# Hybrid two-layer trunk on one core: gate rows by way of DRAM, mLSTM tables with the maximum folded into the forget gate, one decay sum of 129 columns

## The chip, the cores and the metric

The kernel runs on one core of one Trainium2 chip. The metric is the device time of one execution in microseconds (us). The kernel before takes 2866.2 us, the median of three runs (2865.12 to 2867.47 us). Engines are named as the profile names them: PE is TensorE (PEld its weight loads), DVE VectorE, ACT ScalarE, POOL GpSimd, SP SyncE, which issues the DMAs.

## The reference

A trunk of two layers over x, 256 tokens of 2048 channels in float32. Each layer is a token mixer and a SwiGLU feed-forward network (FFN), and each of these four sub-layers ends in the same way:

```python
x = LayerNorm(ALPHA * x + (1 + gate(c)) * f(x * (1 + scale(c)) + shift(c)))
```

Shift, scale and gate are products of SiLU(c) with large modulation weights, 48 tiles of 1 MB for each sub-layer. In layer 0 the mixer is half mLSTM (8 heads of 128 channels) and half RWKV-7 (16 heads of 64), in layer 1 half retention and half gated DeltaNet.

What the change touches is, first, the gate: 2048 numbers, one for each channel, by which every token's row is multiplied. Second, the mLSTM gates. With lf the log-sigmoid of the forget gate and ig the input gate, in the form that both kernels compute:

```python
m[t] = max(lf[t] + m[t-1], ig[t])                      # running maximum, m[-1] = 0
table[s, t] = exp(lf[s+1] + ... + lf[t] + ig[s] - m[t])   # for s <= t
h = (q k^T * table) v / max(|row sum|, exp(-m[t]))
```

Third, RWKV-7's decay: for each channel the running sum of the log decay over time, and the exponentials of it and of its negative.

## The kernel before, in words

Everything stays in one core's on-chip memory but the weights, which stream in once. All large products follow one pattern. A weight tile of 1 MB (`raw`, three buffers) is loaded by SP (L327), split in two halves into a rounded part `hi` on ACT (L340) and the rest `lo` on DVE (L341), and PE multiplies each half by the activations with three matmuls per step (L360 `hi` x high part, L361 `lo` x high part, L362 `hi` x low part), 24 matmuls for a tile, called a unit below. Products gather in the four `g` banks of PSUM. Behind each unit `fill` lets in modulation tiles at a set rate: each is a 1 MB load into a `raw` buffer too, and one DVE pass that multiplies by SiLU(c) and sums (L292).

The other PSUM banks: three `m` banks, used by nearly all small products, and one single `c` bank. The `c` bank serves in turn RWKV's preparation (`rwkv_front`: the decay sum at L741 and the small products behind it), the transposes in front of the causal convolutions (`conv`, L911, two per 512 columns), the retention group's transposes (L1233), and the gate (L320). A tile that is next in line for a bank or buffer waits until the last reader of the tile before has finished. SBUF buffers are handed on in the same way; of the small ones, `t1` has four that go round among many uses (RWKV's state and output tiles, the mLSTM's tables), and `y8` has three of 1 MB (layer-norm sums, `conv` outputs, RWKV's masks, and the gate of 128 x 2048).

Layer 0's mixer is `mixer_ab`: `rwkv` runs four batches of four heads, each a chain of small dependent steps (preparation in `rwkv_front`, triangular inverses L612 to L657, the recurrence up to L823, a normalisation on DVE, L853 to L862), and `mlstm_gates` and two `mlstm_group` follow, each group with two convolutions, the tables of four heads (`mlstm_weights`) and their products. The program is written in this order, but a scheduler in the framework lays the instructions out over the engines: weight tiles are pulled ahead by a priority, and small steps sink in between the product matmuls where their inputs are ready. Each engine then runs its list strictly in order. `mix_out` does the output projection, reads the gate at its start, and ends in the layer norm; `ffn` works in three thirds, and reads the gate before the second third's down projection.

The gate in the kernel before: DVE adds the bias in four pieces, after every fourth modulation tile (L311), giving `one_and_gate`, 128 partitions x 16. `gate_rows` spreads it over all partitions with 16 matmuls (L320), each of one column, repeated 128 times, against the identity; four fill the `c` bank, and ACT copies each bank into the gate tile (L321, four per gate).

The mLSTM table of one head takes five matmuls (L971 to L975): the sums of lf between s and t (L971, L972, L974), and, with 8 rows of the negated maximum and a selecting column, the subtraction of m[t] (L973 on 256 columns, L975 on 128). ACT then takes the exponential with ig as the bias of each row (L977, L978).

The decay sum (L741) multiplies by a constant of 256 columns: the sums up to and with t, and the sums up to but without t. ACT takes the exponential of all 512 results (L744) and of the negative of one half (L746).

Of the kernel before, what the change touches and what calls it, by code (L numbers as in the profile page):

```python
# [19 lines left out]
P = 128  # L20
T = 256
NT = T // P
D = 2048
# [21 lines left out]

CONS = {}
_n = 0
for _name, _w in [("ident", 128), ("cum", 256), ("tr", 128), ("ones", 128), ("sl", 128), ("tri", 32), ("diag", 16), ("blk", 8),
                  ("lev", 64 * len(LEVELS)), ("bones", 128), ("hsel", 2), ("freq", 64)]:
    CONS[_name] = (_n, _w)  # L50
    _n += _w
# [3 lines left out]
def constants():  # L55
    i = np.arange(P)
    c = np.zeros((P, NCONS), np.float32)

    def put(name, a):
        o, w = CONS[name]  # L60
        c[:, o:o + w] = a

    u, t = i[:, None], i[None, :]
    put("ident", np.eye(P))
    after = ((u > 63) & (u <= t)).astype(np.float64) - ((u <= 63) & (u > t))
    before = ((u > 63) & (u < t)).astype(np.float64) - ((u <= 63) & (u >= t))
# [122 lines left out]
class Trunk:  # L189
# [92 lines left out]
    def ada_unit(self, u, deep):  # L282
# [11 lines left out]
        if i < 32:  # L294
# [12 lines left out]
                v.tensor_tensor(bi, bi, sh, ALU.add)  # L307
                v.tensor_tensor(sc, self.cols[:, og:og + 4], sc, ALU.mult)
            return
        if i % 4 == 3:  # L310
            v.scalar_tensor_tensor(self.g1[:, i - 35:i - 31], m[:, i - 3:i + 1], 1.0, self.cols[:, ob + i - 3:ob + i + 1], ALU.add, ALU.add)  # L311

    def gate_rows(self):

        gate = self.y8([P, D])
        for n in range(4):
            b = self.bank("c")
            for j in range(4):
                k = 4 * n + j
                self.nc.tensor.matmul(b[:, P * j:P * j + P], self.g1[:, k:k + 1].to_broadcast([P, P]), self.ident, start=True, stop=True)  # L320
            self.nc.scalar.activation(gate[:, 512 * n:512 * n + 512], b[:], AF.Copy)  # L321
        return gate


# [408 lines left out]
    def rwkv_front(self, B, c):  # L733
# [4 lines left out]
        ar, bk, w = B["ar"], B["bk"], B["w"]  # L738
        b = self.bank("c")
        for t in range(NT):  # L740
            nc.tensor.matmul(b[:, T * t:T * t + T], B["sg"][:, t, P * ct:P * ct + P], self.con("cum"), start=True, stop=True)  # L741
        gg = self.own([P, NT, 2, P], "gg", 1)
        bv = b[:].rearrange("p (t x s) -> p t x s", t=NT, x=2)
        nc.scalar.activation(gg[:], bv, AF.Exp)  # L744
        gi = self.f1([P, NT, P])
        nc.scalar.activation(gi[:], bv[:, :, 0, :], AF.Exp, scale=-1.0)  # L746
        v.reciprocal(B["scol"][:, ct:ct + 1], gg[:, 1, 1, 0:1])
        v.tensor_tensor(B["scol"][:, ct:ct + 1], B["scol"][:, ct:ct + 1], gg[:, 0, 0, P - 1:P], ALU.mult)
# [11 lines left out]
        v.scalar_tensor_tensor(ar[:, ct, :, 0, :], tok(km[:]), self.nkk[:, c:c + 1], gg[:, :, 1, :], ALU.mult, ALU.mult)  # L760
        v.tensor_tensor(ar[:, ct, :, 1, :], tok(rm[:]), gg[:, :, 0, :], ALU.mult)
# [171 lines left out]

    def mlstm_gates(self):

        nc, v, fix = self.nc, self.nc.vector, self.fix
        f = self.g16[:, :, 8:16]
        self.lf = fix.tile([P, NT, 8], F32, name="log_f")
        sp = self.tiny([P, NT, 8])
        self.softplus_neg(sp[:], f, [P, NT, 8])  # L940
        v.tensor_scalar(self.lf[:], f, 0.0, None, ALU.min)
        v.tensor_tensor(self.lf[:], self.lf[:], sp[:], ALU.subtract)
        b = self.bank()
        for t in range(NT):
            nc.tensor.transpose(b[:8, P * t:P * t + P], self.g16[:, t, 0:8], self.ident)
            nc.tensor.transpose(b[:8, T + P * t:T + P * t + P], self.lf[:, t, :], self.ident)
        it = self.t1([8, T])
        v.tensor_copy(it[:], b[:8, 0:T])
        m = self.t1([8, T])
        v.tensor_tensor_scan(m[:], b[:8, T:2 * T], it[:], 0.0, ALU.add, ALU.max)  # L950
        self.mneg = fix.tile([8, T], F32, name="minus_m")
        v.tensor_scalar(self.mneg[:], m[:], -1.0, None, ALU.mult)
        b = self.bank()
        for t in range(NT):
            nc.tensor.transpose(b[:, 8 * t:8 * t + 8], self.mneg[:, P * t:P * t + P], self.ident[:8, :8])
        self.emn = fix.tile([P, NT, 8], F32, name="exp_minus_m")
        nc.scalar.activation(self.emn[:], b[:, 0:16].rearrange("p (t h) -> p t h", t=NT), AF.Exp)

    def mlstm_weights(self, h):

        nc = self.nc
        mm = nc.tensor.matmul
        sl, tr = self.con("sl"), self.con("tr")
        o = CONS["tr"][0]
        tro = self.cons[:, o:o + 256]
# [4 lines left out]
        e = self.ident[:8, h:h + 1].to_broadcast([8, P])  # L970
        mm(b[:, 0:T], L[:, 0, :], tro, start=True, stop=False)  # L971
        mm(b[:, P:T], self.lf[:, 1, h:h + 1].to_broadcast([P, P]), tr, start=False, stop=False)  # L972
        mm(b[:, 0:T], e, self.mneg[:], start=False, stop=True)  # L973
        mm(b[:, T:T + P], L[:, 1, :], tr, start=True, stop=False)  # L974
        mm(b[:, T:T + P], e, self.mneg[:, P:T], start=False, stop=True)  # L975
        E = self.t2([P, 3, P])
        nc.scalar.activation(E[:, 0:2, :], b[:, 0:T].rearrange("p (a t) -> p a t", a=2), AF.Exp, bias=self.g16[:, 0, h:h + 1])  # L977
        nc.scalar.activation(E[:, 2, :], b[:, T:T + P], AF.Exp, bias=self.g16[:, 1, h:h + 1])  # L978
        self.keep_upper(E[:, 0::2, :], [2], False)
        return E  # L980

# [382 lines left out]
```

## Time and profile before

| | |
|---|---|
| median of three runs | 2866.2 us |
| the profiled execution | 2870.56 us |
| its span, first to last instruction | 2868.8 us |
| mean granted TensorE clock | 0.969 of full speed |
| PE busy | 2692.8 us, 94% of the span |
| DVE busy | 2041.5 us, 71% |
| ACT busy | 1263.7 us, 44% |
| POOL busy | 82.5 us, 3% |
| moved by DMA | 674.34 MB, 235 GB/s over the span |

The profile is one execution, cut into views: busy time by engine, groups of equal instructions (busy time, mean of one, and the idle time of the engine ahead of them with what ended it), the busy time of each engine in chosen windows, the timeline, the waits, and the chain of work that ended last. A matmul on 32-bit floats outside the product pattern runs as two records, so 16 matmuls of a gate show as 32, and four gates as 128. A matmul's own time in the records overlaps with that of the next, so what a group of them occupies on PE is read from the starts in the timeline, and is less than the sum of the durations. The profiled execution is 4.4 us longer than the median of the three runs.

### The profile page before, as it was taken

What the parts mean: (1) busy time and instruction counts of PE and PEld (TensorE: products, weight loads), DVE (VectorE), ACT (ScalarE), POOL (GpSimd) and SP (SyncE); (2) the same over time, 40 slices, a digit from 0 to 9 for tenths busy, and PEclk for the clock granted to TensorE, in tenths of its full rate; (3) what the DMA queues carried; (4) which work ended last, traced back from release to release, by engine and by line L of the source; (5) the groups of instructions that cost most, each with busy time, mean ns of one, the idle gap of its engine ahead of it and who ended that gap; (6) DMA issues with size and microseconds to landing.
All of it is one profiled execution on the core that took longest, in us unless ns stands there. A gap on an engine that the chain in (4) does not pass through costs nothing.

```text
span 2868.8 us, 33529 instructions
## 1 busy us (share of the span) xinstructions
PE 2692.8 (94%) x12746; PEld 2215.4 (77%) x12746; DVE 2041.5 (71%) x3255; ACT 1263.7 (44%) x1664; POOL 82.5 (3%) x86
## 2 busy tenths in 40 slices
PE   3699798999899999999998999999989999999997
PEld 2577676777688888888887878787878888888886
DVE  7879677786877557767767898986876545557546
ACT  2264353457354444444444644444444444443442
POOL 0000000011000000000000100101000000000000
PEclk9799798899999999999999999999999999999998
DMA  9977254463568668867855886667656656666553
GB/s 367 354 278 273 92 181 162 181 245 117 197 251 297 249 221 300 301 234 268 298 216 186 296 310 222 247 227 268 222 201 247 235 191 235 235 222 240 193 216 130
DMA packets 106185, 674.34 MB, mean 235 GB/s; under 512 B 12068, under 2 KB 14248, under 8 KB 28328
## 3 DMA queue, kind: packets, MB, share of 16 engines
q1 hardware_dynamic: 106024, 672.20, 64.1%
q8 instruction: 100, 1.64, 0.2%
q14 instruction: 61, 0.50, 0.0%
HBM read 663.77 MB, written 8.39 MB: 234 GB/s over the span
## 4 chain that ended last, share of the span: by engine, by line
PE 77%; DVE 14%; DMA 5%; issue 2%; ACT 2%; POOL 0%; POOLq 0%; SPq 0%; DVEq 0%; ACTq 0%
PE g L361 22%; PE g L362 22%; PE g L360 22%; DVE lo L341 4%; DVE raw L292 4%; DMA raw<-ada 2%; ACT hi L340 1%; PE m L642 1%; PE m L649 1%; DMA raw<-gu 1%; DVE a L292 1%; PE m L793 1%; PE m L578 1%; PE m L656 1%; DMA a<-ada 1%
## 5 line engine op out<-in xcount | busy, mean ns | idle before, releaser
L341 DVE TENSOR_TENSOR lo<-raw,hi 128x1024 fp32r<-128x1024 f32 (+2 forms) x848 | 1022.5, 1211 | 626.4 <-ACT hi L340 623.9
L340 ACT ACTIVATE hi<-raw 128x1024 fp32r<-128x1024 f32 (+2 forms) x848 | 884.4, 1049 | 1164.5 <-PE g L362 931.8
L360 PE MATMUL g<-hi,h 128*128 128x512 f32 (+3 forms) x2368 | 930.0, 395 | 83.4 <-ACT hi L340 77.5
L361 PE MATMUL g<-lo,h 128*128 128x512 f32 (+3 forms) x2368 | 934.5, 395 | 7.4 <-DVE lo L341 7.3
L362 PE MATMUL g<-hi,h 128*128 128x512 f32 (+3 forms) x2368 | 929.8, 393 | 0.0
L360 PEld LDWEIGHTS g<-hi,h 128*128 128x128 f32 x2368 | 452.1, 191 | 178.0 <-ACT hi L340 79.9
L361 PEld LDWEIGHTS g<-lo,h 128*128 128x128 f32 x2368 | 452.5, 191 | 104.0 <-DVE lo L341 16.8
L362 PEld LDWEIGHTS g<-hi,h 128*128 128x128 f32 x2368 | 452.3, 191 | 88.0 <-issue 1.7
L292 DVE SCALAR_TENSOR_TENSOR raw<-raw,silu_c 128x2048 f32<-128x2048 f32 x176 | 405.0, 2302 | 29.7 <-DMA raw<-ada 29.0
L360 PE MATMUL g<-hi,a 128*128 128x512 f32 x960 | 375.2, 391 | 1.1 <-ACT hi L340 1.1
L361 PE MATMUL g<-lo,a 128*128 128x512 f32 x960 | 374.3, 390 | 0.6 <-DVE lo L341 0.6
L362 PE MATMUL g<-hi,a 128*128 128x512 f32 x960 | 374.5, 390 | 0.0
L360 PEld LDWEIGHTS g<-hi,a 128*128 128x128 f32 x960 | 180.2, 188 | 38.5 <-ACT hi L340 1.6
L361 PEld LDWEIGHTS g<-lo,a 128*128 128x128 f32 x960 | 180.3, 188 | 37.8 <-DVE lo L341 0.9
L362 PEld LDWEIGHTS g<-hi,a 128*128 128x128 f32 x960 | 180.2, 188 | 37.0
L918 DVE SCALAR_TENSOR_TENSOR f<-c,cols_sb,f 128x255 f32<-128x255 f32 (+2 forms) x120 | 57.0, 475 | 7.5 <-ACT f L916 6.6
L1115 POOL TENSOR_SCALAR s<-cons_sb,log_alpha 128x128 f32<-128x128 f32 x16 | 18.6, 1177 | 1040.7 <-PE g L362 884.6
L530 ACT ACTIVATE t<-m,affine 128x128 f32<-128x128 f32 x96 | 35.1, 476 | 29.9 <-PE m L527 29.9
L403 ACT ACTIVATE t<-t,affine 128x256 f32<-128x256 f32 x16 | 8.7, 589 | 75.9 <-DVE affine L301 75.9
L292 DVE SCALAR_TENSOR_TENSOR a<-a,silu_c 128x2048 f32<-128x2048 f32 x16 | 36.6, 2287 | 0.4 <-DMA a<-ada 0.3
L527 PE MATMUL m<-cons_sb,y 128*128 128x128 f32 x96 | 16.7, 317 | 18.4 <-DVE v L495 18.4
L662 POOL TENSOR_SCALAR_AFFINE_SELECT a<-a 128x512 f32<-128x512 f32 (+1 forms) x20 | 20.7, 1040 | 454.2 <-ACT a L795 410.1
(386 smaller groups left out, 1966.5 us busy)
## 6 DMA issues: line engine op xcount, KB each, us to landing
raw<-ada SPq DMA_DIRECT2D x176, 1024.0 KB, 5.0
raw<-gu SPq DMA_DIRECT2D x176, 1024.0 KB, 4.9
raw<-dn SPq DMA_DIRECT2D x88, 1024.0 KB, 4.8
raw<-w_cd SPq DMA_DIRECT2D x60, 1024.0 KB, 4.8
raw<-w_ab SPq DMA_DIRECT2D x56, 1024.0 KB, 4.9
a<-ada SPq DMA_DIRECT2D x16, 1024.0 KB, 10.4
raw<-o_ab SPq DMA_DIRECT2D x16, 1024.0 KB, 4.8
raw<-o_cd SPq DMA_DIRECT2D x16, 1024.0 KB, 4.8
```

The lines of the kernel that those rows point to most:

```text
L292: v.scalar_tensor_tensor(w[:], w[:], 1.0, self.sc[:], ALU.mult, ALU.mult, accum_out=m[:, i:i + 1])
L340: nc.scalar.activation(hi[:, :2 * n], ws, AF.Copy)
L341: nc.vector.tensor_tensor(lo[:, :2 * n], ws, hi[:, :2 * n], ALU.subtract)
L360: mm(o, ah, wh, start=first, stop=False)
L361: mm(o, ah, wl, start=False, stop=False)
L362: mm(o, al, wh, start=False, stop=stop and k == 3)
L530: nc.scalar.activation(h32[:, j, :], b[:, P * j:P * j + P], AF.Identity, bias=self.ab[:, 16 + k:17 + k], scale=self.ab[:, k:k + 1])
L578: nc.tensor.transpose(b[:, P * k:P * k + P], gs[:, t, P * k:P * k + P], self.ident)
L642: nc.tensor.matmul(x[:, 64 * j:64 * j + 64], mt[:, hs.start + j, :], dv[:, hs.start + j, :, 0, :], start=True, stop=True)
L649: nc.tensor.matmul(x[:, 256 + 64 * j:320 + 64 * j], dt[:, hs.start + j, :], y[:, j, :], start=True, stop=True)
L656: nc.tensor.transpose(x[:, P * j:P * j + P], d[:, hs.start + j, :], self.ident)
L918: v.scalar_tensor_tensor(o[:, d:T], z[:, 0:T - d], self.col(wname, c + 3 - d), o[:, d:T], ALU.mult, ALU.add)
```

## The change

Four edits.

The gate: when the last modulation tile of a sub-layer is done, one DVE instruction adds the biases to all 16 columns. PE transposes them into 16 rows of 128 in the `c` bank (L312), ACT copies the rows into a `t1` tile (L314), and SP writes these 8 KB to DRAM (L316). `gate_rows` is then one DMA that reads the row of 2048 numbers into all 128 partitions of the gate tile, 1 MB (L321). Line numbers of the changed kernel differ by one or a few from those of before.

The mLSTM gates: `lf` becomes lf[t] + m[t-1] - m[t], and the input gate becomes ig[t] - m[t], both formed on 8 rows before they are transposed back. The sums over the new lf then hold the subtraction of the maximum, and the two matmuls of 8 rows fall away in each head. The first matmul's second half now takes the constant of ones in place of a table that ran on into it; six transposes of 8 rows (L961) go back where two went, ACT copies two of the three results and takes the exponential of the negative of the third.

The decay sum: one constant of 129 columns, the first of them the sum up to the chunk's start. Columns 0 to 127 are then the sums without t, columns 1 to 128 those with t, and ACT takes the exponential of 258 results.

```diff
-put("cum", DECAY * np.concatenate([after, before], 1))
+put("cum", DECAY * np.concatenate([-(u <= 63).astype(np.float64), after], 1))
...
-        if i % 4 == 3:
-            v.scalar_tensor_tensor(self.g1[:, i - 35:i - 31], m[:, i - 3:i + 1], 1.0, self.cols[:, ob + i - 3:ob + i + 1], ALU.add, ALU.add)
+        if i == 47:
+            v.scalar_tensor_tensor(self.g1[:], m[:, 32:48], 1.0, self.cols[:, ob + 32:ob + 48], ALU.add, ALU.add)
+            b = self.bank("c")
+            nc.tensor.transpose(b[:16, 0:P], self.g1[:], self.ident)
+            row = self.t1([16, P])
+            nc.scalar.activation(row[:], b[:16, 0:P], AF.Copy)
+            self.gate_row = self.dram.tile([16, P], F32, name=self.name("gate_row"))
+            nc.sync.dma_start(self.gate_row[:], row[:])
 
     def gate_rows(self):
 
         gate = self.y8([P, D])
-        for n in range(4):
-            b = self.bank("c")
-            for j in range(4):
-                k = 4 * n + j
-                self.nc.tensor.matmul(b[:, P * j:P * j + P], self.g1[:, k:k + 1].to_broadcast([P, P]), self.ident, start=True, stop=True)
-            self.nc.scalar.activation(gate[:, 512 * n:512 * n + 512], b[:], AF.Copy)
+        self.nc.sync.dma_start(gate[:], self.gate_row[:].rearrange("k p -> (k p)").unsqueeze(0).to_broadcast([P, D]))
         return gate
...
-            nc.tensor.matmul(b[:, T * t:T * t + T], B["sg"][:, t, P * ct:P * ct + P], self.con("cum"), start=True, stop=True)
-        gg = self.own([P, NT, 2, P], "gg", 1)
+            nc.tensor.matmul(b[:, (P + 1) * t:(P + 1) * (t + 1)], B["sg"][:, t, P * ct:P * ct + P], self.con("cum"), start=True, stop=True)
+        gg = self.own([P, NT, P + 1], "gg", 1)
...
-        self.mneg = fix.tile([8, T], F32, name="minus_m")
-        v.tensor_scalar(self.mneg[:], m[:], -1.0, None, ALU.mult)
+        v.tensor_tensor(it[:], it[:], m[:], ALU.subtract)
+        fm = self.t1([8, T])
+        v.tensor_tensor(fm[:, 1:T], b[:8, T + 1:2 * T], m[:, 0:T - 1], ALU.add)
+        v.tensor_copy(fm[:, 0:1], b[:8, T:T + 1])
+        v.tensor_tensor(fm[:], fm[:], m[:], ALU.subtract)
         b = self.bank()
-        for t in range(NT):
-            nc.tensor.transpose(b[:, 8 * t:8 * t + 8], self.mneg[:, P * t:P * t + P], self.ident[:8, :8])
...
+        for j, x in enumerate((fm, it, m)):
+            for t in range(NT):
+                o = 16 * j + 8 * t
+                nc.tensor.transpose(b[:, o:o + 8], x[:, P * t:P * t + P], self.ident[:8, :8])
...
-        mm(b[:, 0:T], L[:, 0, :], tro, start=True, stop=False)
-        mm(b[:, P:T], self.lf[:, 1, h:h + 1].to_broadcast([P, P]), tr, start=False, stop=False)
-        mm(b[:, 0:T], e, self.mneg[:], start=False, stop=True)
-        mm(b[:, T:T + P], L[:, 1, :], tr, start=True, stop=False)
-        mm(b[:, T:T + P], e, self.mneg[:, P:T], start=False, stop=True)
+        mm(b[:, 0:P], L[:, 0, :], tr, start=True, stop=True)
+        mm(b[:, P:T], L[:, 0, :], self.con("ones"), start=True, stop=False)
+        mm(b[:, P:T], self.lf[:, 1, h:h + 1].to_broadcast([P, P]), tr, start=False, stop=True)
+        mm(b[:, T:T + P], L[:, 1, :], tr, start=True, stop=True)
```

How the order moves is shown on two engines, PE at two places and ACT at one. Rows carry the source line, the operation, and the tiles by the program's names; "x4" is four alike in a row.

PE, where RWKV's third batch ends in layer 0's mixer, kernel before: `c_3481` and `c_3498` are convolution transposes, `m_2624` and `m_2629` the batch's output transposes and gate products, `g_3866` a product bank.

```order
L822 MATMUL m_2509<-q_2155,a_2281 128x64
L823 MATMUL m_2509<-s_2559,a_2281 128x64
L774 MATMUL c_2908<-cons_sb,z_2836 128x128 x2
L776 MATMUL c_2908<-cons_sb,y_2812 128x128 x2
L360 MATMUL g_3866<-hi_3984,h_674 128x512
L361 MATMUL g_3866<-lo_3985,h_674 128x512
L362 MATMUL g_3866<-hi_3984,h_674 128x512
L911 MATMUL c_3481<-cons_sb,zt_3478 128x128 x4
L911 MATMUL c_3498<-cons_sb,zt_3478 128x128 x4
L853 MATMUL m_2624<-cons_sb,t_2615 128x128
L861 MATMUL m_2629<-q_839,q_2145 128x256
```

The same place in the changed kernel:

```order
L822 MATMUL m_2507<-q_2153,a_2279 128x64
L312 MATMUL c_3446<-cons_sb,one_and_gate 16x128
L814 MATMUL m_2544<-s_2551,y_2332 128x64 x4
L823 MATMUL m_2507<-s_2557,a_2279 128x64
L822 MATMUL m_2507<-q_2153,a_2279 128x64
L823 MATMUL m_2507<-s_2557,a_2279 128x64
L821 MATMUL m_2507<-s_2538,y_2152 128x128
L822 MATMUL m_2507<-q_2153,a_2279 128x64
L823 MATMUL m_2507<-s_2557,a_2279 128x64
L822 MATMUL m_2507<-q_2153,a_2279 128x64
L823 MATMUL m_2507<-s_2557,a_2279 128x64
L853 MATMUL m_2622<-cons_sb,t_2613 128x128
```

The gate's transpose now takes the `c` bank inside the recurrence, no product matmul stands between the batch's last steps, and the convolution transposes are gone from here.

PE, the first mLSTM head's table, kernel before: `m_4022` is the table's bank, `m_4032` the bank of the scores.

```order
L362 MATMUL g_4729<-hi_4844,h_674 128x512
L955 MATMUL m_3321<-cons_sb,minus_m 128x8 x2
L971 MATMUL m_4022<-cons_sb,s_4019 128x256
L972 MATMUL m_4022<-cons_sb,log_f 128x128
L973 MATMUL m_4022<-minus_m,cons_sb 128x256
L974 MATMUL m_4022<-cons_sb,s_4019 128x128
L975 MATMUL m_4022<-minus_m,cons_sb 128x128
L985 MATMUL m_4032<-y_3326 128x256
L986 MATMUL m_4032<-y_3326 128x128
L360 MATMUL g_4729<-hi_4844,h_674 128x512
```

The same table in the changed kernel, from the last gate product of RWKV's fourth and last batch (`m_3261`) on; L946, L947 and L961 are the transposes of the mLSTM gates, `c_3492` a convolution's.

```order
L862 MATMUL m_3261<-q_839,q_2800 128x256
L947 MATMUL m_3307<-cons_sb,v_3278 8x128
L946 MATMUL m_3307<-cons_sb,gates 8x128
L947 MATMUL m_3307<-cons_sb,v_3278 8x128
L911 MATMUL c_3492<-cons_sb,zt_3489 128x128 x4
L961 MATMUL m_3321<-cons_sb,s_3317 128x8 x2
L961 MATMUL m_3321<-cons_sb,s_3312 128x8 x2
L961 MATMUL m_3321<-cons_sb,s_3314 128x8 x2
L977 MATMUL m_4033<-cons_sb,s_4030 128x128
L978 MATMUL m_4033<-cons_sb,s_4030 128x128
L979 MATMUL m_4033<-cons_sb,mlstm_gates 128x128
L980 MATMUL m_4033<-cons_sb,s_4030 128x128
```

Four matmuls stand where five stood, and gates and table now follow on the end of RWKV's last batch, with the first convolution's transposes between and no product matmul; in the order before, some 90 product matmuls stand between that batch's output (L853) and this table.

ACT, changed kernel, around the row copy of the first gate: `s_3448` is the row tile, `s_3262` and `s_3270` are outputs of RWKV's fourth batch.

```order
L858 ACTIVATE s_3262<-m_3256,cols_sb 128x256
L858 ACTIVATE s_3270<-m_3256,cols_sb 128x256
L314 ACTIVATE s_3448<-c_3446 16x128
L916 ACTIVATE f_3497<-c_3492,cols_sb 128x256
L964 ACTIVATE mlstm_gates<-m_3321 128x32
```

The copy that frees the `c` bank stands behind the end of RWKV's fourth batch, one batch after the transpose that fills it, because the `t1` tile that it writes is free only then; the first convolution (L916) follows at once.

More of the change, by code (lines that the diff above doesn't have):

```diff
@@ L937, in mlstm_gates @@
         f = self.g16[:, :, 8:16]
-        self.lf = fix.tile([P, NT, 8], F32, name="log_f")
+        lf = self.tiny([P, NT, 8])
         sp = self.tiny([P, NT, 8])
         self.softplus_neg(sp[:], f, [P, NT, 8])
-        v.tensor_scalar(self.lf[:], f, 0.0, None, ALU.min)
-        v.tensor_tensor(self.lf[:], self.lf[:], sp[:], ALU.subtract)
+        v.tensor_scalar(lf[:], f, 0.0, None, ALU.min)
+        v.tensor_tensor(lf[:], lf[:], sp[:], ALU.subtract)
         b = self.bank()
@@ L945, in mlstm_gates @@
             nc.tensor.transpose(b[:8, P * t:P * t + P], self.g16[:, t, 0:8], self.ident)
[L946 removed]
+            nc.tensor.transpose(b[:8, T + P * t:T + P * t + P], lf[:, t, :], self.ident)
         it = self.t1([8, T])
@@ L950, in mlstm_gates @@
         v.tensor_tensor_scan(m[:], b[:8, T:2 * T], it[:], 0.0, ALU.add, ALU.max)
-        self.mneg = fix.tile([8, T], F32, name="minus_m")
-        v.tensor_scalar(self.mneg[:], m[:], -1.0, None, ALU.mult)
-        b = self.bank()
-        for t in range(NT):
-            nc.tensor.transpose(b[:, 8 * t:8 * t + 8], self.mneg[:, P * t:P * t + P], self.ident[:8, :8])
-        self.emn = fix.tile([P, NT, 8], F32, name="exp_minus_m")
-        nc.scalar.activation(self.emn[:], b[:, 0:16].rearrange("p (t h) -> p t h", t=NT), AF.Exp)
+        v.tensor_tensor(it[:], it[:], m[:], ALU.subtract)
[3 more added lines that the diff above has]
+        v.tensor_tensor(fm[:], fm[:], m[:], ALU.subtract)
+        b = self.bank()
+        for j, x in enumerate((fm, it, m)):
+            for t in range(NT):
+                o = 16 * j + 8 * t
+                nc.tensor.transpose(b[:, o:o + 8], x[:, P * t:P * t + P], self.ident[:8, :8])
+        three = fix.tile([P, 3, NT, 8], F32, name="mlstm_gates")
+        self.lf, self.im, self.emn = (three[:, j] for j in range(3))
+        nc.scalar.activation(three[:, 0:2], b[:, 0:32].rearrange("p (x t h) -> p x t h", x=2, t=NT), AF.Copy)
+        nc.scalar.activation(self.emn, b[:, 32:48].rearrange("p (t h) -> p t h", t=NT), AF.Exp, scale=-1.0)
     def mlstm_weights(self, h):
```

22 lines of the change are left out of this document (9 added, 13 removed).

## Prediction

> **What bounds the kernel now.** I read the page's busy times first, then the groups of PE, then windows along the span, to see where PE is fed and where not.
>
> ```profile
> PE 2692.8 (94%) x12746; PEld 2215.4 (77%) x12746; DVE 2041.5 (71%) x3255; ACT 1263.7 (44%) x1664; POOL 82.5 (3%) x86
> PE 77%; DVE 14%; DMA 5%; issue 2%; ACT 2%; POOL 0%; POOLq 0%; SPq 0%; DVEq 0%; ACTq 0%
> ```
>
> PE is busy for 94% of the span and carries 77% of the chain that ended last. So a matmul taken away shortens the run wherever PE has no waits, and only there. The windows tell where that is. In each row stand the stretch, its length, then busy time and count for PE, PEld, DVE, ACT and POOL, and the granted clock (then DMA share and GB/s).
>
> ```profile
> 424.00:453.00 29.00, 22.07 (x87) 16.75 (x85) 25.58 (x85) 13.40 (x21) 2.25 (x3) 0.82 0.44 163
> 453.00:492.00 39.00, 38.98 (x286) 35.52 (x284) 25.52 (x61) 16.05 (x28) 0.00 (x0) 1.00 0.46 162
> 500.00:517.00 17.00, 15.76 (x50) 9.85 (x51) 7.20 (x23) 8.79 (x27) 1.63 (x3) 0.59 0.08 33
> 592.00:635.00 43.00, 42.72 (x193) 33.34 (x191) 40.47 (x101) 24.02 (x35) 6.09 (x2) 1.00 0.72 268
> 635.00:660.00 25.00, 21.43 (x82) 16.22 (x83) 12.48 (x25) 13.01 (x19) 11.00 (x14) 0.80 0.48 170
> 660.00:735.00 75.00, 73.82 (x368) 59.18 (x367) 54.33 (x146) 50.11 (x75) 5.01 (x10) 1.00 0.41 141
> 1237.00:1244.00 7.00, 7.00 (x53) 6.29 (x52) 3.82 (x6) 3.79 (x6) 0.00 (x0) 1.00 0.67 252
> 1768.00:1812.00 44.00, 43.67 (x213) 36.70 (x212) 36.96 (x95) 22.91 (x35) 5.12 (x8) 0.92 0.53 192
> 1976.00:2015.00 39.00, 38.69 (x200) 32.66 (x200) 20.12 (x34) 16.88 (x23) 0.00 (x0) 1.00 0.61 222
> 2559.00:2567.00 8.00, 8.00 (x57) 6.97 (x55) 3.85 (x6) 4.72 (x7) 0.00 (x0) 1.00 0.38 131
> ```
>
> The two FFN gates (1237 to 1244, 2559 to 2567) and layer 1's mixer gate (inside 1976 to 2015) lie where PE has no hole. Layer 0's mixer (424 to 735) is mixed: the small RWKV steps of 453 to 492 and of 592 to 635 are filled up with products, while at 424 to 453, around 500, and at 635 to 660 PE stands still for some microseconds and the clock falls.
>
> **What comes off PE.** A gate costs four groups of four matmuls (eight records). One timeline row folds such a group, and the start of the next row tells how long it holds PE.
>
> ```profile
> 1237.17 0.39 PE L362 MATMUL g<-hi,h 128*128 128x512 f32 x1
> 1237.40 1.05 PE L320 MATMUL c<-cons_sb,one_and_gate 128*128 128x128 f32 x8
> 1238.29 0.60 PE L578 MATMUL m<-cons_sb,q 128*128 128x128 f32 x4
> ...
> 1239.40 1.06 PE L320 MATMUL c<-cons_sb,one_and_gate 128*128 128x128 f32 x8
> 1240.21 0.48 PE L361 MATMUL g<-lo,a 128*128 128x512 f32 x1
> ```
>
> The first holds it for 0.89 us, the second for 0.81: 3.4 us per gate. The one transpose that stays is a quarter of a group, 0.2 us. So 3.2 us go per gate, 12.8 for four; the group rows bound this from above, 17.9 us of busy time.
>
> ```profile
> L320 PE MATMUL c<-cons_sb,one_and_gate 128*128 128x128 f32 x128 | 17.9, 277 | 0.0
> L741 PE MATMUL c<-cons_sb,b 128*128 128x256 f32 x32 | 10.3, 445 | 0.0
> L973 PE MATMUL m<-minus_m,cons_sb 8*128 8x256 f32 x16 | 6.1, 461 | 0.0
> L975 PE MATMUL m<-minus_m,cons_sb 8*128 8x128 f32 x16 | 4.2, 343 | 0.0
> L972 PE MATMUL m<-cons_sb,log_f 128*128 128x128 f32 x16 | 3.3, 292 | 0.0
> 660.01 0.60 PE L971 MATMUL m<-cons_sb,s 128*128 128x256 f32 x2
> 660.45 0.38 PE L972 MATMUL m<-cons_sb,log_f 128*128 128x128 f32 x2
> 660.76 0.69 PE L973 MATMUL m<-minus_m,cons_sb 8*128 8x256 f32 x2
> 661.39 0.49 PE L974 MATMUL m<-cons_sb,s 128*128 128x128 f32 x2
> 661.80 0.48 PE L975 MATMUL m<-minus_m,cons_sb 8*128 8x128 f32 x2
> 662.22 0.70 PE L985 MATMUL m<-y 128*128 128x256 f32 x2
> ```
>
> A table: from 660.01 to 662.22 five matmuls hold PE for 2.21 us. Four of 128 columns stand there afterwards; those of this head start 0.31 (L972) and 0.41 us (L974) before their successors, so the four take 1.24 to 1.64, and a head saves 0.57 to 0.97 us, eight heads 4.6 to 7.8. The busy times of L973 and L975 make 10.3. Four transposes more cost some 0.4. I take 7.
>
> The decay sum: 129 columns aren't in the trace; the nearest row is one of 128. By mean durations 445 − 292 = 153 ns go per record, 4.9 us over 32; by starts 0.44 − 0.31 = 0.13 us per matmul, 2.1 over 16. I take 3. ACT's exponential over 258 in place of 512 numbers, 12 bias additions fewer on DVE, three small DVE operations more among the mLSTM gates and 16 gate copies fewer on ACT cost PE nothing by themselves: in these stretches DVE and ACT have time left.
>
> Together PE loses 6.4 (FFN gates) + 3.2 (layer 1's gate) + 13.2 (layer 0: 3.2 + 3 + 7) = 22.8 us of work.
>
> **What the new path adds.** The gate's transpose needs the only `c` bank, and the copy that frees it needs a `t1` tile. In layer 0 that copy stands behind the last output of RWKV's fourth batch. Queued behind the held bank on PE are the mLSTM convolutions (L911), and behind them the convolutions' DVE and ACT work. The order shows two places where PE is then left without products.
>
> First, the third batch's small steps, which the kernel before mixes with products in 453 to 492 (16 matmuls of L362, so 48 in all):
>
> ```profile
> 453.00:492.00 39.00, 7.07 (x16) 3.04 (x16) 1.00 0.46 162
> L911 PE MATMUL c<-cons_sb,zt 128*128 128x128 f32 x80 | 14.1, 291 | 7.7 <-DVE v L418 7.6
> 316.19 0.47 PE L853 MATMUL m<-cons_sb,t 128*128 128x128 f32 x1 [7.97 <-ACT t L848]
> ```
>
> At 0.23 us from start to start (1237.17 to 1237.40) the 48 are 11.0 us. They now run ahead of the batch, where PE stood idle for 6.9 us (29.00 − 22.07) that they can fill; inside the batch nothing covers them. That adds 11.0 − 6.9 = 4 at most, and I take 3. The 7.7 us wait before L911 goes, but the batch's normalisation is next there: before the first batch's L853 PE waited 7.97 us for it. That is no change.
>
> Second, the end of the fourth batch. Its normalisation was covered before (592 to 635, PE 42.72 of 43.00). Now the batch's output, the gates of the mLSTM and the first table follow on each other without products: 8.0 us for the normalisation by the row above, and the chain of the gates, which took 6.1 us from its transposes to the tables:
>
> ```profile
> L946 PE MATMUL m<-cons_sb,log_f x2: 272/272/272, 628.8 to 629.0; 128*8 128x128 f32 x2
> 634.90 0.29 PE L955 MATMUL m<-cons_sb,minus_m 8*128 8x8 f32 x2
> ```
>
> Part of those two run side by side, and the products moved away from here (some 19 between the recurrence and the output, 4.4 us) are in the first figure's favour; the idle 3.6 us of 635 to 660 (25.00 − 21.43) go. 8.0 + 6.1 − 4.4 − 3.6 = 6.1; I take 6, with bounds of 0 (DVE gets through before PE has run dry) and 17.
>
> The clock: after the wait at 500 it was 0.59 for 17 us, which is 7.0 us of lost clock; a wait at the fourth batch's end brings a stretch like it, and the one at 635 to 660, 25 us at 0.80 or 5.0, goes. That is +2. The Trainium skill, "TensorE: Matmul & The Clock Gate", section "HAM oscillation — how this bites in real kernels", says that a gap of more than about 3.4 us without matmuls puts the clock back to half; this trace agrees (7.7 us without, then 0.59). By that rule alone, with no credit for 635 to 660, the term would be 7 and the sum 5 us higher.
>
> In layer 1 the held bank delays the convolutions of the second DeltaNet group, and the group's decay tables and triangular set-up stand at one place without products, where the kernel before has 43.67 us of PE in 44.00 with products between. POOL scales the group's eight tables there, in two fours:
>
> ```profile
> L1115 POOL TENSOR_SCALAR s<-cons_sb,log_alpha 128x128 f32<-128x128 f32 x16 | 18.6, 1177 | 1040.7 <-PE g L362 884.6
> ```
>
> 1.18 us each, 4.7 for a four and 9.4 for both. I take 4, one four bare, between 0 and 9. So layer 1 is 3.2 saved against 4 given back.
>
> The DMAs: SP writes 8 KB and reads 1 MB per gate, in its queue ahead of weight loads. The nearest rows:
>
> ```profile
> x<-y SPq DMA_DIRECT2D x24, 256.0 KB, 2.9
> a<-lnrow SPq DMA_DIRECT2D x2, 1024.0 KB, 7.3
> raw<-dn SPq DMA_DIRECT2D x88, 1024.0 KB, 4.8
> ```
>
> 2.9 + 7.3 = 10.2 us from the write's issue to the gate. In three of the four cases several weight loads lie between write and read. In the last FFN they follow on each other, and SP holds the next weights back while it waits for the write. Three `raw` buffers are 3 x 24 x 0.23 = 16.6 us of PE work, so 10.2 is covered; with one buffer full (5.5 us) 4.7 would show. I take 0.
>
> The sum: −22.8 + 3 + 6 + 2 + 4 = −7.8 us. The profiled execution's 2870.56 becomes 2862.8; it stands 4.4 us above the median of the runs, so 2866.2 becomes 2858.4, say 2858.
>
> **The rivals.** Runs of this kernel lie 2.4 us apart, and 0.2%, 5.7 us, is about what a measurement can tell from no change. With 22.8 us taken off PE, it is faster if less than 17.1 us come back as waits, and slower if more than 28.5 do.
>
> *All of it comes through* (0.18). DVE and ACT keep ahead, the waits at the bare stretches only take the place of those that the trace has at 500 and 635. For it speaks that DVE is busy for only 12.48 of 25.00 at 635 to 660; against it, that it is busy for 40.47 of 43.00 in 592 to 635, where the deferred convolutions would now compete. 2866.2 − 22.8 = 2843; with the busy times of the rows, 17.9 + 10.3 + 4.9 = 33, it would be 2833.
>
> *The held `c` bank starves PE* (0.19). The convolutions come up to eight product units late, the first head waits for them, and DVE is handed the end of the batch, the gates and the convolutions at once while PE has nothing. Price: 4 at the third batch, 17 at the fourth (8.0 + 6.1 uncovered, and a further 3 for one convolution's DVE steps in front of the first scores), a half-clock stretch of 7 behind it, and 9 in layer 1: 37. 2866.2 − 22.8 + 37 = 2880. It decides from 28.5 us of waits on.
>
> *The two cancel* (0.22). Waits of 17.1 to 28.5 us in the two mixers eat what the FFNs and the tables give: 2866, within 5.7.
>
> *The gate by way of DRAM is late* (0.04). If SP's wait leaves one weight tile ahead, 4.7 us show at each of two to four gates: about 2867 to 2877 with my other terms. Against it: before, SP itself waited over a millisecond in all for `raw` buffers to come free, so the loads are ahead of their use as a rule.
>
> ```profile
> SPq L327 <- DVE lo L341: 1311.8, 330, 16.3
> ```
>
> **How the numbers follow.** My forecast, waits of about 15 us (7 to 17), has 0.37. Faster by over 0.2%: 0.37 + 0.18 = 0.55, and 0.01 for a late gate beside an otherwise free gain, 0.56. Within 0.2%: 0.22 + 0.02 = 0.24. Slower: 0.19 + 0.01 = 0.20. The range goes from 2837, which leaves the lower half of the free gain's own spread out, to 2874, which leaves half of the starved case out.
>
> **What would show it right or wrong.** In the changed profile the FFN gates have no eight-record rows in the `c` bank, and the stretches around 1237 and 2559, counted from one layer norm to the next, are shorter by 3.2 us each: if not, the premise that PE has no hole there is wrong. In layer 0's mixer PE's busy time falls by about 13 us and the mixer's length by less; windows at the ends of the third and fourth batch show PE at a good half of the time and the clock down. If PE is as full there as before, the first rival holds; if they show over 28 us of new idle time, the second. A wait of `hi` for a `dn` load near the last gate would show the fourth. What would make the forecast wrong as a whole is the order's bare places costing nothing, or each costing twice what I took.

## The result, and the profile after

The changed kernel is slower: 2885.34 us, median of four runs (2882.09 to 2889.13), against 2866.39 us before (four runs, 2865.12 to 2867.47). The ratio is 1.0068, with a 95% interval of 1.0053 to 1.0082. The forecast was 2858 us with a range of 2837 to 2874. The rival that came true is the second: the held `c` bank starves PE, put at 2880 us and a chance of 0.19.

The first lines of the page after:

```profile
span 2880.4 us, 33289 instructions
...
PE 2680.6 (93%) x12610; PEld 2205.3 (77%) x12610; DVE 2044.6 (71%) x3246; ACT 1258.2 (44%) x1654; POOL 79.0 (3%) x86
```

PE executes 136 records fewer and its busy time falls by 12.2 us (2692.8 − 2680.6), while the span grows by 11.6. The work did go, then, and waits and slow clock took its place. The groups that answer to those of before:

```profile
L911 PE MATMUL c<-cons_sb,zt 128*128 128x128 f32 x80 | 14.5, 300 | 8.4 <-DVE f L918 6.4 <-ACT s L314 2.0
L741 PE MATMUL c<-cons_sb,b 128*128 128x129 f32 x32 | 6.2, 309 | 1.5 <-ACT b L778 1.5
L977 PE MATMUL m<-cons_sb,s 128*128 128x128 f32 x16 | 3.5, 302 | 1.0 <-POOL s L975 1.0
L978 PE MATMUL m<-cons_sb,s 128*128 128x128 f32 x16 | 3.3, 292 | 0.0
L979 PE MATMUL m<-cons_sb,mlstm_gates 128*128 128x128 f32 x16 | 3.3, 293 | 0.0
L980 PE MATMUL m<-cons_sb,s 128*128 128x128 f32 x16 | 3.3, 293 | 0.0
L312 PE MATMUL c<-cons_sb,one_and_gate 128*16 128x128 f32 x4 | 1.1, 273 | 0.4 <-DVE one_and_gate L310 0.4
```

The gate's 17.9 us are 1.1, the decay sum's 10.3 are 6.2, and the four table matmuls together 13.4. The new thing is in the first row's last columns: the convolutions' transposes wait for L314, the gate's row copy.

Where the time went is read by counting product matmuls, of which both kernels run the same 10,176. The table gives the start of the one that opens the unit named (24 to a unit), taken from the trace of one execution each.

| unit | place | before, us | after, us | later by |
|---|---|---|---|---|
| 51.9 | fourth RWKV batch's recurrence is over | 588.3 | 593.2 | 5.0 |
| 52.1 | next unit | 589.4 | 624.3 | 34.9 |
| 75.9 | end of layer 0's mixer | 775.9 | 783.1 | 7.3 |
| 156.0 | gate of the first FFN | 1238.6 | 1244.6 | 6.0 |
| 160.0 | behind it | 1263.8 | 1268.0 | 4.2 |
| 234.0 | second DeltaNet group | 1689.2 | 1692.8 | 3.6 |
| 248.1 | behind its set-up | 1807.8 | 1825.4 | 17.5 |
| 268.0 | ahead of layer 1's mixer gate | 1957.0 | 1970.3 | 13.3 |
| 280.0 | behind it | 2037.9 | 2048.8 | 10.9 |
| 370.0 | ahead of the last FFN's gate | 2548.6 | 2563.3 | 14.7 |
| 376.0 | behind it | 2585.9 | 2597.1 | 11.2 |

Two places lose: the fourth batch's end, where 30 us come at once and part is made good by unit 76, and the second DeltaNet group. They are the two bare places of the order that lie behind the gate's transpose. Three gates gain, 1.8, 2.4 and 3.5 us. Another 3.8 us are lost between units 280 and 370 (14.7 − 10.9); what takes them stays open. The windows of the two losing places, in the columns used before:

```profile
593.00:624.00 31.00, 13.51 (x45) 7.88 (x44) 20.12 (x69) 11.71 (x26) 6.17 (x11) 0.59 0.28 103
1801.00:1826.00 25.00, 16.06 (x63) 11.89 (x63) 22.66 (x65) 10.20 (x16) 9.18 (x10) 0.66 0.47 168
```

PE is busy for 13.51 of 31.00 us in the first and for 16.06 of 25.00 in the second, and the granted clock is 0.59 and 0.66. In the kernel before the first place was full (592 to 635: 42.72 of 43.00). PE's timeline there, from the last product on:

```profile
593.69 0.39 PE L362 MATMUL g<-hi,h 128*128 128x512 f32 x1
600.61 0.47 PE L853 MATMUL m<-cons_sb,t 128*128 128x128 f32 x1 [6.53 <-ACT t L848]
...
606.56 1.22 PE L861 MATMUL m<-q,q 128*128 128x256 f32 x2 [2.31 <-DVE s L863]
...
611.64 1.11 PE L911 MATMUL c<-cons_sb,zt 128*128 128x128 f32 x4 [1.99 <-ACT s L314]
612.69 0.80 PE L961 MATMUL m<-cons_sb,s 8*128 8x8 f32 x6
614.49 0.79 PE L977 MATMUL m<-cons_sb,s 128*128 128x128 f32 x2 [0.99 <-POOL s L975]
...
615.92 0.63 PE L980 MATMUL m<-cons_sb,s 128*128 128x128 f32 x2
621.17 1.08 PE L911 MATMUL c<-cons_sb,zt 128*128 128x128 f32 x4 [4.62 <-DVE f L918]
623.31 0.80 PE L360 MATMUL g<-hi,h 128*128 128x512 f32 x1 [1.05 <-ACT zt L698]
```

From 593.69 to 623.31 no product runs. The waits follow one another: the normalisation (6.53), the batch's output (2.31, while DVE works through a modulation pass of 2.28 us that stands ahead in its list), the held bank (1.99), POOL's scaling (0.99), and 4.62 for the convolution that was held back. With the 1.05 ahead of the first product they are the 17.5 us that PE was idle (31.00 − 13.51). The 4.62 come from the single bank again: the second pair of transposes needs it, and ACT and DVE must read it out first. ACT's second copy of it (L916) stands behind the first table's exponentials and a table load. ACT's timeline shows this, and what held the bank before:

```profile
604.53 0.56 ACT L858 ACTIVATE s<-m,cols_sb 128x256 f32<-128x256 f32 x1
611.33 0.27 ACT L314 ACTIVATE s<-c 16x128 f32<-16x128 f32 x1 [6.24 <-DVE a L391]
612.79 0.47 ACT L916 ACTIVATE f<-c,cols_sb 128x256 f32<-128x256 f32 x1 [1.20 <-PE c L911]
...
617.03 0.36 ACT L983 ACTIVATE t<-m,mlstm_gates 128x128 f32<-128x128 f32 x1
617.40 1.28 ACT L920 ACT_TABLE_LOAD   x1
618.70 0.42 ACT L920 ACTIVATE y<-f 128x256 f32<-128x256 f32 x1
619.02 0.46 ACT L916 ACTIVATE f<-c,cols_sb 128x256 f32<-128x256 f32 x1
```

The row copy stands idle for 6.24 us until DVE's L391, the last reader of the fourth batch's output, lets go of a `t1` tile. The transpose that filled the bank had run at 498.1:

```profile
L312 PE MATMUL c<-cons_sb,one_and_gate x4: 271/272/277, 498.1 to 2574.2; 128*16 128x128 f32 x4
```

So the bank was held from 498 to 611, for 113 us, for a copy of 0.27. The first convolution's transposes run at 611.6 us, against 492.1 in the kernel before. In layer 1 the same transpose and copy stand 55 us apart, and there ACT did not even stand idle ahead of the copy:

```profile
1687.63 0.28 PE L312 MATMUL c<-cons_sb,one_and_gate 128*16 128x128 f32 x1 [0.36 <-DVE one_and_gate L310]
1742.56 0.25 ACT L314 ACTIVATE s<-c 16x128 f32<-16x128 f32 x1
```

### The profile page after: what moved, and what is told of

It reads as the page before. It is cut to its first block, busy times and chain, and to the rows that moved or that the text cites. A ratio compares the mean times of both kernels' runs of the same rounds, so it can differ in the third digit from the quotient of the medians.

```text
span 2880.4 us, 33289 instructions
## 1 busy us (share of the span) xinstructions
PE 2680.6 (93%) x12610; PEld 2205.3 (77%) x12610; DVE 2044.6 (71%) x3246; ACT 1258.2 (44%) x1654; POOL 79.0 (3%) x86
## 4 chain that ended last, share of the span: by engine, by line
PE 58%; DVE 8%; DMA 4%; issue 1%; ACT 1%; POOL 0%; POOLq 0%; DVEq 0%; ACTq 0%
PE g L361 18%; PE g L362 18%; PE g L360 18%; DVE lo L341 3%; DMA raw<-ada 2%; DVE raw L291 2%; DMA raw<-gu 1%; ACT hi L340 1%; PE m L578 1%; PE m L527 0%; DMA t<-x 0%; DMA t<-lnrow 0%; PE m L642 0%; PE m L649 0%; DVE f L918 0%
## 5 line engine op out<-in xcount | busy, mean ns | idle before, releaser
L918 DVE SCALAR_TENSOR_TENSOR f<-c,cols_sb,f 128x255 f32<-128x255 f32 (+2 forms) x120 | 57.2, 477 | 12.4 <-ACT f L916 11.2
```

The costliest lines, as they stand in the source:

```text
L918: v.scalar_tensor_tensor(o[:, d:T], z[:, 0:T - d], self.col(wname, c + 3 - d), o[:, d:T], ALU.mult, ALU.add)
```

## The experiments

Medians in us; "before" was run beside each set (2865.4, 2865.5 and 2865.3 us).

| run | what it has | median | ratio, 95% interval |
|---|---|---|---|
| e1_gate_only | gate edit | 2886.2 | 1.0070 [1.0055, 1.0085] |
| e2_cum_only | decay sum | 2870.8 | 1.0024 [1.0008, 1.0039] |
| e3_tables_only | mLSTM tables | 2860.4 | 0.9979 [0.9970, 0.9989] |
| e4_own_row | all, own row tile | 2854.3 | 0.9964 [0.9945, 0.9982] |
| e5_no_cum_own_row | gate with own row tile, tables | 2863.8 | 0.9999 [0.9989, 1.0009] |
| e6_own_row_layer0 | all, own row tile in the first gate | 2864.5 | 0.9992 [0.9978, 1.0006] |
| e7_tables_and_cum | tables, decay sum | 2863.2 | 0.9994 [0.9982, 1.0007] |
| e8_late_row | all, row made where the gate is read | 2851.1 | 0.9950 [0.9935, 0.9965] |
| e9_m_bank_t1_row | all, transpose in an `m` bank | 2857.1 | 0.9973 [0.9959, 0.9987] |
| e10_late_no_cum | late row, tables | 2857.9 | 0.9977 [0.9962, 0.9991] |

The theory after the result (A): the gate's transpose holds the single `c` bank until its row copy gets a `t1` tile; the convolutions behind it come late, and PE runs out of products at two places. The rivals: the round trip through DRAM costs the time (B), or the order of the third RWKV batch, which stands without products since the shorter decay sum (C).

**Each edit alone.** The gate alone, the diff's part in `ada_unit` and `gate_rows`:

```diff
-        if i % 4 == 3:
+        if i == 47:
...
+        self.nc.sync.dma_start(gate[:], self.gate_row[:].rearrange("k p -> (k p)").unsqueeze(0).to_broadcast([P, D]))
```

> Only the gate edit (transpose, row copy, DRAM write, broadcast read); tables and decay sum as before. Theory A (the gate's transpose holds the single c bank until its row copy gets a t1 tile, which delays the convolutions and leaves PE without products at the end of the fourth RWKV batch and in the second DeltaNet group): the FFNs give back 4.9 us, layer 0 loses about 9 net and layer 1 about 9 net, as in the changed kernel, so about 2879 us (2874 to 2884). Theory B (the DRAM round trip and SP's waits cost the time): the same total, but with waits of hi for weight loads near the four gates. Theory C (the loss is the order of the third RWKV batch, which the shorter decay sum brings about): about 2856 us, since the gate alone then only saves.

It measured 2886.2 us, above the range that A gave it: the gate edit by itself loses as much as the whole change, and C is out as the main cause. A and B are not told apart by it. The gate's DMAs held SP for little: of the changed kernel's waits on SP's queue (total us, times, longest) the gate's are these.

```profile
SPq L316 <- ACT s L314: 8.3, 3, 5.7
SPq L316 <- ACT s L1176: 4.2, 1, 4.2
SPq L321 <- DMA gate_row<-s: 3.1, 1, 3.1
```

SP waited 3.1 us in all for a write to land, once of four times, and 12.5 us for row copies, against over a millisecond for `raw` buffers before. So the trace leaves B little room. The decay sum alone, then the tables alone:

```diff
-            nc.tensor.matmul(b[:, T * t:T * t + T], B["sg"][:, t, P * ct:P * ct + P], self.con("cum"), start=True, stop=True)
+            nc.tensor.matmul(b[:, (P + 1) * t:(P + 1) * (t + 1)], B["sg"][:, t, P * ct:P * ct + P], self.con("cum"), start=True, stop=True)
```

> Only the decay sum of 129 columns; gate and tables as before. In its order the third batch's small steps stand without products, as in the changed kernel, which loses 5.0 us up to the fourth batch's end. Theory A: that place costs about what it cost there, 5 us, and nothing else changes: about 2871 us (2867 to 2875). Theory C: this place is the main loss, over 2875 us. If bare places cost nothing: 3 us less PE work, 2863 us.

```diff
-        mm(b[:, 0:T], e, self.mneg[:], start=False, stop=True)
...
-        mm(b[:, T:T + P], e, self.mneg[:, P:T], start=False, stop=True)
```

> Only the mLSTM gates and tables with the maximum in the forget gate; gate and decay sum as before. All theories: PE loses about 7 us of work in layer 0 (4.6 to 10.3) and the order has no new bare place but the first table: about 2860 us (2855 to 2865). If the work taken off is covered by other waits there: 2866.

They measured +5.4 and −4.9 us, both as expected. The third batch's bare place comes with the decay sum and not with the held bank, to which the prediction had put it: with the decay sum alone the last unit ahead of the place (43.9) starts at 456.2 us, 34.9 earlier than before, and the next (44.1) at 527.8, 16.0 later; with the gate alone they start 8.3 and 11.9 later, with the products still between the batch's steps. In the changed kernel PE was busy for 36.39 of the 39.00 us from 463 to 502, at a granted clock of 0.79: small steps, not idle time, fill the place. The first batch has such a place too: at units 32 and 44 no product starts for 64 to 74 us in every traced kernel with the short decay sum, against 43 to 52 and 19 to 23 us in those without.

**The row tile.**

```diff
-            row = self.t1([16, P])
+            row = self.own([16, P], "gr", 1)
```

> The whole change, but the row copy writes a tile of its own and not one of the four t1 tiles, so that the c bank is held only for the transpose and the copy. Theory A: the two bare places at the fourth batch's end and in layer 1 are gone; 12.5 and 12 us come back, and what stays is the third batch's place: about 2860 us (2852 to 2865). Theory B: the DRAM path is unchanged, so 2880 us or more. Theory C: the third batch's place is unchanged, so 2880 us or more.

2854.3 us, as A had it: 31 less than the changed kernel, by one line that changes no arithmetic and no DMA. B and C both said 2880 or more. The stretch that held the bare place, in this kernel:

```profile
600.00:632.00 32.00, 32.00 (x146) 24.92 (x145) 30.89 (x82) 18.25 (x32) 0.00 (x0) 1.00 0.87 320
```

PE is full and at full clock, and DVE is busy for 30.89 of 32.00: its steps no longer stand alone. The split by place:

```diff
-            row = self.t1([16, P])
+            row = self.own([16, P], "gr", 1) if sub == 0 else self.t1([16, P])
```

> The whole change, with a row tile of its own for the first gate alone; the other three rows go to t1 as in the changed kernel. Theory A: layer 0's place at the fourth batch's end is mended, layer 1's is not: 2854.3 plus the 12 us of layer 1, about 2866 us (2860 to 2871). If layer 0's place was all of the loss: 2854.

2864.5 us, within A's range. By the medians layer 1's place is worth 10.2 us (2864.5 − 2854.3) and layer 0's 20.8 (2885.3 − 2864.5). By the traces of single executions it is 11.3 for layer 1 (from 12.7 us ahead of the kernel before at unit 207.9 to 1.4 ahead at 291.9) and 13.7 for layer 0 (7.3 later against 6.4 earlier at 75.9), so layer 0's price is known only to some 7 us. The stretches in which no product starts say the same without a price. One of 29.6 us at unit 52 and one of 23.1 at 248 stand in the changed kernel. Both are in e1 (29.5 and 22.8), the second alone in e6 (22.7), and neither, nor any over 5 us at these units, in the kernel before, e2 to e5 and e7 to e10.

**Bank or tile?**

```diff
-            b = self.bank("c")
+            b = self.bank()
```

> The whole change, but the gate's transpose takes one of the three m banks in place of the single c bank; the row copy still writes a t1 tile and still waits for one. If the held c bank was the loss (theory A as narrowed by the runs so far): like the mended kernel, 2851 to 2857 us. If the wait for the t1 tile by itself was the loss (ACT's queue stands behind the copy): still over 2870 us.

2857.1 us, the upper end of what the held bank as the cause allows. With the row still in a `t1` tile, but another bank, the loss is gone. In this kernel's order the transpose itself moves too (in layer 0 to unit 58, in layer 1 to 246), and the copies start within 3.6 us of it. So the run shows that the gate with a `t1` row does no harm out of the `c` bank; whether a long wait for the tile would do harm by itself, by holding up ACT's list, it does not show. In layer 1 of the changed kernel such a wait is ruled out, since ACT was not idle ahead of the copy.

**What the gate by way of DRAM is worth.** First the other two edits with the old gate, against the changed kernel:

```diff
-        self.nc.sync.dma_start(gate[:], self.gate_row[:].rearrange("k p -> (k p)").unsqueeze(0).to_broadcast([P, D]))
+                self.nc.tensor.matmul(b[:, P * j:P * j + P], self.g1[:, k:k + 1].to_broadcast([P, P]), self.ident, start=True, stop=True)
```

> Tables and decay sum as in the changed kernel, gate as before (64 matmuls, 16 copies). Against the whole change with a row tile of its own this prices the gate by way of DRAM with nothing held: if the 3.2 us of PE work per gate come through, 2854.3 plus 12.8, about 2867 us (2862 to 2870); by the two edits run alone, 2865.4 plus 5.4 less 4.9, 2866 us. If the DRAM path has costs of its own that eat the saving: 2856 or less.

With the old gate beside the other two edits the time is 2863.2 us. So the new gate, with nothing held, is worth 8.9 us (2863.2 − 2854.3), against 12.8 forecast; the intervals do not tell the two apart. Made late, it is worth 12.1 (2863.2 − 2851.1); these lines then stand in `gate_rows` and no more in `ada_unit`:

```diff
...
+        b = self.bank("c")
+        nc.tensor.transpose(b[:16, 0:P], self.g1[:], self.ident)
+        row = self.own([16, P], "gr", 1)
+        nc.scalar.activation(row[:], b[:16, 0:P], AF.Copy)
+        self.gate_row = self.dram.tile([16, P], F32, name=self.name("gate_row"))
+        nc.sync.dma_start(self.gate_row[:], row[:])
         gate = self.y8([P, D])
         self.nc.sync.dma_start(gate[:], self.gate_row[:].rearrange("k p -> (k p)").unsqueeze(0).to_broadcast([P, D]))
```

> The whole change, but transpose, row copy and DRAM write are made where the gate is read and not when the last modulation tile is done, with a row tile of its own: the bank is held only briefly and late, and the DRAM write, its landing and the 1 MB read stand in SP's queue right before the gate is needed. Theory A: like the mended kernel, about 2854 us (2849 to 2860). Theory B (the round trip through DRAM is long enough to be seen): over 2860 us, with PE waiting for hi, or DVE for the gate, behind each of the four gates.

2851.1 us, as A had it, where B asked for over 2860. It is the fastest of all, though not apart from 2854.3 by the intervals. Here the round trip stands right before its use, and is still covered. The median times to landing in this kernel (KB each, us):

```profile
y<-gate_row SPq DMA_DIRECT2D x4, 1024.0 KB, 6.8
gate_row<-gr SPq DMA_DIRECT2D x4, 8.0 KB, 4.7
```

**The decay sum's price.** Two runs were to fix it: the kernel with a row tile of its own (e4) and the late one (e8), each with the old decay sum.

```diff
-            nc.tensor.matmul(b[:, (P + 1) * t:(P + 1) * (t + 1)], B["sg"][:, t, P * ct:P * ct + P], self.con("cum"), start=True, stop=True)
+            nc.tensor.matmul(b[:, T * t:T * t + T], B["sg"][:, t, P * ct:P * ct + P], self.con("cum"), start=True, stop=True)
```

> Gate by way of DRAM with a row tile of its own, and the mLSTM tables; the decay sum as before, with 256 columns. Theory A (row tile and held bank were the loss; the decay sum's order at the third RWKV batch costs about 5 us): 2854.3 less 5.4, about 2849 us (2845 to 2853). If the decay sum is neutral in company of the other edits: 2854 (2852 to 2857).

> Tables, and the gate made late with a row tile of its own; the decay sum as before. Of the runs so far two bear on the decay sum against each other: alone it cost 5.4 us, in company of the mended gate and the tables it gained 9.5. If the order of the first RWKV batch decides (in both kernels with the new gate and the old decay sum that batch ended 6 to 9 us late): again late there, about 2860 us (2855 to 2865). If the decay sum has a price of its own: 2851.1 less 5.4, about 2846 us.

Without the decay sum e4's kernel takes 2863.8 us (9.5 more than with it), which neither of the two cases had, and the late one 2857.9 (6.8 more), where the order of the first RWKV batch had put it. With the old gate the decay sum costs 5.4 alone and 2.8 beside the tables (2863.2 − 2860.4), the latter within the intervals. By these medians its sign depends on the gate's edit. That the order of the first RWKV batch decides it is not shown, though: PE, DVE and ACT run the same order in e9 as in e4 up to 500 us, and yet e9's traced execution, 9.7 us above that kernel's median, was as late behind that batch as e5 and e10 were (unit 32.1 at 349.1 us, against 346.5 and 346.6, and 342.4 in e4). The two kernels' windows over that batch, e4's and then e9's:

```profile
290.00:342.00 52.00, 40.56 (x202) 32.28 (x203) 26.73 (x100) 19.94 (x52) 3.93 (x5) 0.66 0.13 46
```

```profile
290.00:342.00 52.00, 44.90 (x204) 37.27 (x203) 22.54 (x74) 17.98 (x47) 2.46 (x3) 0.61 0.13 47
```

The same order of instructions, at a clock of 0.66 in one and 0.61 in the other (e9's window ends a little earlier in it): from 275.5 (e4) and 275.3 us (e9), where unit 31.9 starts, unit 32 starts at 341.4 and at 348.1. A single trace can therefore not price an edit of 5 us in this mixer, and why the decay sum helps one gate and hurts the other stays open.

## Why the prediction was wrong, point by point

**Bounds.** PE as the bound, and the FFN gates and layer 1's gate as places without holes, held. The last FFN's gate gave 3.5 us (14.7 − 11.2), layer 1's 2.4 (13.3 − 10.9), the first FFN's 1.8 (6.0 − 4.2), 7.7 in all against the 9.6 that the prediction took for these three.

**What came off.** The tables gave 4.9 us alone (interval 3.2 to 8.6) and 7.6 beside the decay sum (2870.8 − 2863.2), where 7 was taken: right as far as the runs tell. The decay sum, −3 and a bare place of +3, was forecast at nothing and measured +5.4 alone, with an interval that begins at +0.08%; this term's size and its dependence on the gate were missed, and its bare place was put down to the wrong edit.

**The step that failed** is the price of "the end of the fourth batch": "8.0 + 6.1 − 4.4 − 3.6 = 6.1; I take 6". The mechanism was there, the held bank, the copy behind the fourth batch, the convolutions behind it. The size was not: with 2 for the clock it was 8, and the runs made it 20.8 by the medians, 13.7 by the traces. Three things in it were wrong, as the timeline after shows. It credited 4.4 us of products as moved ahead, but unit 52.1, which opened at 589.4 us ahead of the batch's end, opened at 624.3 behind it. (The slow clock of 635 to 660 did go, and part of the idle time with it: from 640 to 735 PE was busy for 92.65 of 95.00 us at a clock of 1.00, in the kernel before for 95.26 of 100.00 from 635 on, at 0.95.) It took the normalisation and the gates, 14.1 us, as the whole, where the convolutions follow in the same gap: from the first table's last row to the second convolution's transposes it is 621.17 − 615.92 = 5.3 us. And it took the slow clock as a stretch of its own behind the gap, where the gap itself ran at 0.59, its small dependent matmuls included.

**Layer 1** was the same error: "one four bare", 4 us, from POOL's rows, where the runs gave 10.2. By the profile none of PE's waits from 1801 to 1826 ended on POOL: of 8.9 us, 5.7 ended on DVE (L918, L1131) and 3.3 on ACT. DVE was busy for 22.66 of the 25.00 us, with three modulation passes (6.9), the convolutions' L918 (5.7) and the products with the decay tables (L1130 and L1131, 4.3) as the largest parts. The upper bound of 9 was near.

**The sum** over the two places is 31.0 us against 12 forecast (6 + 2 + 4). With them taken out, the whole change is −11.1 us (2854.3 − 2865.4), against −19.8 in the forecast (−22.8 + 3). So of the 28 us between forecast and measurement 19 lie in these two terms and 9 in the savings.

**The rivals.** The second, 37 us of waits and 2880, has the mechanism: its 17 + 7 for the fourth batch's end stand against 20.8, and its 9 for layer 1 against 10.2. That its total is only 5 us off is in part luck, since it took all of the 22.8 us off and 4 us for the third batch, which the gate alone does not bring. Its chance of 0.19 was too low: the order had shown both bare places beforehand. What the prediction weighed was DVE's share in the stretches before, 12.48 of 25.00 us and 40.47 of 43.00. In the bare place DVE was busy for 20.12 of 31.00: it had time left, but its steps stood one behind the other. The fourth rival, a late gate, did not occur: PE waited nowhere for it, and around the last gate (2560 to 2620) `hi` waited for no load.

**The clock rule.** The Trainium skill, "TensorE: Matmul & The Clock Gate", section "HAM oscillation — how this bites in real kernels", puts the clock to half after some 3.4 us without matmuls; the trace after agrees at the fourth batch's end (6.5 us without matmuls up to 600.61, a clock of 0.50 from 599.0 to 629.4). The sum 5 us higher that it gave in the prediction was still too low, as the gap was. In layer 1 no such gap stands ahead, and the clock fell all the same:

```profile
1801.00:1807.00 6.00, 3.41 (x21) 2.52 (x21) 5.73 (x19) 4.09 (x6) 1.57 (x2) 1.00 0.57 188
1807.20:1824.10 16.90, 10.54 (x32) 7.59 (x32) 15.26 (x42) 6.11 (x10) 7.07 (x8) 0.50 0.48 179
```

PE was busy for 3.41 of 6.00 us ahead of the fall, and its longest wait there was 1.01 us. So small matmuls with short waits between them brought the clock down here without one long gap, and the measurement decides.

## What to carry to other kernels

Where a pool has one buffer, ask of each new user not how long it works but until when it holds the buffer, and that is set by what its last reader waits for: here a copy of 0.27 us kept the bank for 113 us because its output came out of a ring shared with RWKV's fourth batch. A place in the new order where many small dependent steps stand without filler work is better priced as the whole chain to the next filler at the slow clock, and work counts as moved ahead only where the order shows it ahead; here that chain was 29.6 us at 0.59. A tile of its own for a small long-lived value was worth 31 us here.

## What the runs showed of the hardware that was not expected

The slow clock in a run of small matmuls is not the same from one execution to the next. Over the first RWKV batch's end two kernels with the same order there were 6.7 us apart (341.4 and 348.1 us at unit 32), at granted clocks of 0.66 and 0.61. The runs of one kernel lie up to 22 us apart, and with the decay sum alone the time goes with the mean granted clock, from 2860.2 us at 0.971 to 2882.4 at 0.963. The spread of 2.4 us that the prediction took from three runs of the kernel before was luck; 29 later ones spread over 16.8. That is why the ratios above have intervals of 0.2 to 0.4% and why one profile of such a mixer shows places, not prices. Also, the same 8 KB write that took 4.7 us to land in e8 had a median of 1.3 in the changed kernel, and the 1 MB read 9.4 against 6.8; the runs don't show why.

```profile
y<-gate_row SPq DMA_DIRECT2D x4, 1024.0 KB, 9.4
gate_row<-s SPq DMA_DIRECT2D x4, 8.0 KB, 1.3
```
